# A memset moved to GpSimd and low parts moved between engines in a fused encoder block

## The chip, the cores and the metric

The kernel runs on one core of one Trainium2 chip. The metric is the device time of one execution in microseconds (us), the median of several runs. TensorE does the matrix products, VectorE and ScalarE the elementwise work, GpSimd a little of both, and SyncE issues most of the loads. Each engine has a queue of its own instructions, which run in the order that the program gives them, and waits for the others by semaphores.

## The reference, cut to what matters

One layer of a residual block on x of 512 tokens by 1024 features, all in float32:

```python
h = rms_norm(x, attn_norm_g);  z = h @ w_in
y_mla  = mla_group(...)     # 8 latent-attention heads of width 64, chunked causal mask
y_diff = diff_group(...)    # 4 differential heads of width 128:
#   logits_m = q_m @ k_m.T * 64**-0.5 + bias[head, key - query]; masked by chunks of 64 frames
#   attn = softmax(logits_0) - lam * softmax(logits_1);  o = rms_norm(attn @ v) * (1 - lam_init)
x = x + concat([y_mla, y_diff]) @ w_out
x = x + (silu(causal_conv3(h2 @ w_gate)) * (h2 @ w_up)) @ w_down      # h2 = rms_norm(x)
x = x + sigmoid(rms_norm(x) @ w_ple_gate) * (p @ w_ple_proj)          # p: 512 x 256
```

## The kernel before, in words

**Products in three parts.** Each float32 operand is held as a high part, a cast to a shorter format by ScalarE, and a low part, operand minus high part. `mm3` (lines 155 to 157) adds three TensorE products: high by high, high by low, low by high. For a weight, `load_w` loads a raw tile of 128 x 1024 (`raw`, three buffers), lets ScalarE cast it (`S.copy`, line 148) and subtracts on VectorE or, if `eng` says so, on another engine (line 149). `split` (lines 189, 190, 192, 193) does the same for other tiles. A raw buffer comes free for the next load when its low part is done.

**The order of attention.** Heads are worked through in 32 slots (8 latent heads, 4 query blocks of 128 rows each), then 16 slots (4 differential heads, 4 query blocks). In a latent slot, `mla_logits` multiplies, VectorE takes the negated row maximum (`nm`, line 562) and scales it (line 563), ScalarE takes the exponential (`pm`, line 565), `probs_T` transposes on TensorE (line 530) and copies out (`pt`, lines 533 and 535), and `mla_pv` multiplies by the values (line 575). In a differential slot VectorE adds the bias in one pass (line 667), ScalarE exponentiates (line 668), and VectorE combines the two maps (lines 672 to 674). Between these steps `pump` puts pieces of other work: the projections for the differential heads (`zd`) during the latent heads, the output projection's first half (`wo_units(0, ...)`, tiles `o`) during the differential ones. TensorE's order is that of the code; those of VectorE, ScalarE and GpSimd are set by a scheduler in this part, and by the code before the fifth slot and in the FFN.

**The bias strip.** `bias_strip` is called in the seventh slot. GpSimd builds a row of biases per head (line 593), writes it to memory, spreads it over 128 rows, and reads it back shifted by one element per row (line 598), which gives the tile `strip`, 128 x 4 x 512. Then line 599 sets a corner of it, 64 rows by 4 x 64, to a large number: the part of the mask within the diagonal block. The strip is read from the first differential slot on (line 667).

**The output projection.** `wo_units(kq, dqs, nk)` loads and splits its weights through `wo_w`. For `kq` 0 the low parts are on VectorE; for `kq` 1, whose two weights are loaded during the last latent head and the differential heads, they are on GpSimd. The last two weights (`dq` 2 and 3) take the default, VectorE. The result is added to x by VectorE (`add_x`, line 623). At a head's end `diff_pv` normalises it (`yd`, lines 688 to 698, the last of them the multiplication), and `y_split` transposes it (`yT`, line 609) for the output projection.

**p.** After attention's code, two more tiles are split into `pk`: p transposed (`pT`) and half of its projection weights (`pp0`). They go through the same raw buffers. The products that read `pk` come after the output projection.

Of the kernel before, what the change touches and what calls it, by code (L numbers as in the profile page):

```python
# [15 lines left out]
ALU = mybir.AluOpType  # L16
# [10 lines left out]
MASK = 1e30  # L27
# [62 lines left out]
def _f32(ap):  # L90
    return ap.bitcast(F32)
# [3 lines left out]
def hybrid_block(ctx: ExitStack, tc: tile.TileContext, a: dict, out: bass.AP):  # L95
    nc = tc.nc
    V, S, G, TE = nc.vector, nc.scalar, nc.gpsimd, nc.tensor
# [11 lines left out]
    def bank(tag, name):  # L109
        return pp_.tile([P, 512], F32, tag=tag, bufs={"acc": 2, "lg": 3, "tp": 2, "ob": 1}[tag], name=name)  # L110
# [4 lines left out]
    def sq_tile(name):  # L115
        return att.tile([P, D], F32, tag="sq", bufs=2, name=name)

    def pm_tile(name):
        return att.tile([P, T], F32, tag="pm", bufs=PM, name=name)
# [4 lines left out]
    def xn_tile(name):  # L124
        return keep.tile([P, D], F32, tag="xn", bufs=4, name=name)
# [7 lines left out]
    def small(name, shape, pool=None):  # L133
        return (pool or att).tile(shape, F32, name=name)
# [3 lines left out]
    def load_raw(src, n, name):  # L138
        raw = wp["rawpool"].tile([P, 1024], F32, tag="raw", bufs=wp["raw"], name=f"raw_{name}")
        nc.sync.dma_start(raw[:, :n], src)  # L140
        return raw

    def load_w(src, n, name, eng=None):

        raw = load_raw(src, n, name)
        hi = wp["pool"].tile([P, 1024], F32R, tag="hi", bufs=wp["w"], name=f"hi_{name}")
        lo = wp["pool"].tile([P, 1024], F32R, tag="lo", bufs=wp["w"], name=f"lo_{name}")
        S.copy(hi[:, :n], raw[:, :n])
        (eng or V).tensor_tensor(lo[:, :n], raw[:, :n], _f32(hi[:, :n]), op=ALU.subtract)
        return hi, lo  # L150

    def mm3(ps, blocks, first=True, last=True, again=False):
        n = len(blocks)
        for i, (xh, xl, wh, wl) in enumerate(blocks):
            TE.matmul(ps, xh, wh, start=first and i == 0, stop=False, skip_group_check=again)  # L155
            TE.matmul(ps, xh, wl, start=False, stop=False, skip_group_check=again)  # L156
            TE.matmul(ps, xl, wh, start=False, stop=last and i == n - 1, skip_group_check=again)  # L157
# [28 lines left out]
    def split(h_, l_, src, col=None, eng=None):  # L186

        if col is None:
            S.copy(h_, src)  # L189
            return (eng or V).tensor_tensor(l_, src, _f32(h_), op=ALU.subtract)  # L190
        else:
            S.activation(h_, src, AF.Identity, scale=col)
            return V.scalar_tensor_tensor(l_, src, col, _f32(h_), op0=ALU.mult, op1=ALU.subtract)
# [58 lines left out]
    for kq in range(4):  # L252
        raw = xn_tile(f"xT{kq}")
# [71 lines left out]
    raw, ukv_ = load_raw(a["w_ukv"], 1024, "ukv"), []  # L325
# [259 lines left out]
    def bias_strip():  # L585

        tab = small("tab", [DH, 32])
        nc.sync.dma_start(tab, a["rel_bias"])
        vec1 = dram.tile([DH, NR], F32, name="vec1")
        vec2 = dram.tile([P, DH, NR], F32, name="vec2")  # L590
        vb = sq_tile("vb")[:DH, :NR]
        for c0, c1, b in RUNS:
            G.tensor_scalar(vb[:, c0:c1], tab[:, b:b + 1].broadcast_to([DH, c1 - c0]), -1.0, None, op0=ALU.mult)
        nc.gpsimd.dma_start(vec1, vb)
        nc.gpsimd.dma_start(vec2, vec1.partition_broadcast(P))
        strip = att.tile([P, DH, T], F32, tag="strip", name="strip")
        skew = bass.AP(vec2.tensor, vec2.offset + 127, [[DH * NR - 1, P], [NR, DH], [1, T]])
        nc.gpsimd.dma_start(strip, skew)
        V.memset(strip[:64, :, 448:], MASK)
        strips.append(strip)  # L600


# [10 lines left out]
    def wo_blocks(k0, k1, b, w):  # L613

        c = [slice((k % 4) * 256 + (b % 2) * P, (k % 4) * 256 + (b % 2) * P + P) for k in range(k0, k1)]
        return [(w[0][:, c[i]], w[1][:, c[i]], yh[k0 + i], yl[k0 + i]) for i in range(k1 - k0)]
# [5 lines left out]
    def add_x(b, ps):  # L622
        V.tensor_tensor(xb(b), xb(b), ps, op=ALU.add)  # L623

    wo2 = {}

    def wo_w(kq, dq, eng=None):
        return load_w(a["w_out"][kq, dq], 1024, f"o{kq}{dq}", eng)

    def wo_units(kq, dqs, nk):  # L630

        for dq in dqs:
            w = wo_w(kq, dq, G if kq else V)
            if kq:
                wo2[dq] = w
            for b in (2 * dq, 2 * dq + 1):
                ps = bank("acc", f"o{kq}{b}")
                for k in range(0, nk, 2):
                    mm3(ps, wo_blocks(4 * kq + k, 4 * kq + k + 2, b, w), k == 0, k == nk - 2)
                    if k == nk - 2:  # L640
                        add_x(b, ps)
                    yield

    df = {}
# [9 lines left out]
    def diff_logits(h, t):  # L654
        n = (t + 1) * P
        if t == 0:
            df["s0", h] = sm.tile([P, NT], F32, tag="s0", name="s0")
        s0 = df["s0", h][:, t:t + 1]
        (qh_, ql_), (kh_, kl_) = df["qk", h, 0], df["qk", h, 1]
        pms, s1 = [], sm.tile([P, 1], F32, tag="s1", bufs=4, name="s1")  # L660
        for m in range(2):
            r = slice(64 * m, 64 * m + 64)
            ps = bank("lg", f"dl{h}{t}{m}")
            mm3(ps[:, :n], [(qh_[r, tsl[t]], ql_[r, tsl[t]], kh_[r, :n], kl_[r, :n])])
            pm = pm_tile("pmd")
            nm = sm.tile([P, 1], F32, tag="nm", bufs=4, name="nmd")
            V.tensor_tensor_reduce(out=pm[:, :n], in0=ps[:, :n], in1=strips[0][:, h, T - n:], scale=1.0, scalar=3e38, op0=ALU.add, op1=ALU.min, accum_out=nm)
            S.activation(pm[:, :n], pm[:, :n], AF.Exp, bias=nm, scale=-1.0, accum_out=s0 if m == 0 else s1)
            pms.append(pm)

        cf = sm.tile([P, 1], F32, tag="cf", bufs=4, name="cf")
        V.reciprocal(cf, s1)
        V.scalar_tensor_tensor(cf, cf, nlam, s0, op0=ALU.mult, op1=ALU.mult)
        V.scalar_tensor_tensor(pms[0][:, :n], pms[1][:, :n], cf, pms[0][:, :n], op0=ALU.mult, op1=ALU.add)
        df["pm", h, t] = pms[0]

    def diff_pv(h, t):
# [43 lines left out]
    for i, (h, t) in enumerate(slots):  # L721
        if i + 1 < len(slots):
            mla_logits(*slots[i + 1])
        if i == 4:
            region.__exit__(None, None, None)
        if i == 8:
            with tc.issue_after(mla["k"].ins):
                zd_norm(0)
        if h + 1 < H and t < 2:
            (mla_q, mla_k)[t](h + 1)  # L730
        if i < 3:
            zw1.append(load_w(a["w_d"][1, i + 1], 1024, f"d1{i + 1}"))
        if h < H - 1:
            pump(FILL_MLA[t])
        if i == 6:
            bias_strip()
        if h == H - 1:
            if t == 0:
                pump(100)
                fill.append(wo_units(0, range(4), 4))  # L740
            last_mla[t]()
        mla["pt", h, t] = probs_T(mla.pop(("pm", h, t)), t, f"m{h}{t}", t % 2)
        if i:
            mla_pv(*slots[i - 1])
    diff_logits(0, 0)
    mla_pv(*slots[-1])
    diff_logits(0, 1)
    pump()
    y_split(3, ymn[3], None, "tp")
    for i, (h, t) in enumerate(dslots):  # L750
        if i + 2 < len(dslots):
            diff_logits(*dslots[i + 2])
        if h + 1 < DH and t == 0:
            diff_T(h + 1, 1)
        pump(FILL_DIFF[h][t])
        df["pt", h, t] = probs_T(df.pop(("pm", h, t)), t, f"d{h}{t}", True)
        if i:
            diff_pv(*dslots[i - 1])
        if h + 1 < DH and t == 0:
            diff_T(h + 1, 0)  # L760
        if h and t == 3:
            y_split(4 + h - 1, df["y", h - 1], ocol, "tp")
            if h == 2:
                fill.append(wo_units(1, range(2), 2))
# [7 lines left out]
    for dq in (2, 3):  # L772
        wo2[dq] = wo_w(1, dq)

    pk = kvp.tile([P, 4, 1024], F32R, tag="kv", name="pk")
    for i, (src, name) in enumerate(((a["pT"], "pT"), (a["w_pp"][0], "pp0"))):
        split(pk[:, 2 * i], pk[:, 2 * i + 1], load_raw(src, 1024, name))
    ptw, wpp = (pk[:, 0], pk[:, 1]), [(pk[:, 2], pk[:, 3])]
    order = (0, 4, 1, 5, 2, 6, 3, 7)
    early = {}  # L780
    for b in order[:6]:
        n = len(early)
# [464 lines left out]
```

## Time and profile before

| | |
|---|---|
| time, median of 3 runs | 681.25 us (681.24 to 685.42) |
| profiled execution | 685.5 us, its span 683.7 us |
| TensorE busy | 654.0 us, 96% of the span |
| VectorE busy | 487.9 us, 71% |
| ScalarE busy | 358.2 us, 52% |
| GpSimd busy | 60.5 us, 9% |
| mean granted TensorE clock | 0.979 of full speed |

In the profile PE is TensorE, PEld its weight loads, DVE VectorE, ACT ScalarE, POOL GpSimd, SP SyncE; a letter q behind a name means the engine's issue queue. L599 is line 599. Rows of the time order read: start, length, engine, line, operation, output <- inputs, and in brackets how long the engine had been idle before and what released it. Rows of the list of waits read: who waited, for whom, us in total, times, longest. Rows of the chain read: start, length, engine, tile, line, where "issue" is time in which the profile shows nothing that was waited for. In tables of stretches each engine's busy time is followed by its number of instructions; the last three columns are the granted clock (1.00 is full speed), the share of the DMA engines in use, and GB/s. Attention's slots run from about 70 to 250 us, the FFN from there to the end.

### The profile page before, as it was taken

Reading aid. Unit: us, or ns where it says so; the run is one execution under the profiler, and the core shown is the slowest. Engines: PE = TensorE matmul, PEld = TensorE weight load, DVE = VectorE, ACT = ScalarE, POOL = GpSimd, SP = SyncE. Lnnn points to the kernel's source line nnn. Section 1 sums busy time; section 2 is a strip of 40 time slices with the busy share of each in tenths; the row PEclk is TensorE's granted clock in tenths of the full one; section 3 lists DMA queues with packets and bytes.
Section 4 is the critical chain, followed back from the end, with each engine's and each line's share of the span. In section 5 each row is a group of like instructions: output and inputs, shape, how many; then the busy total and the mean of one; then the engine's idle time right before and its main releaser. Section 6 shows DMA issues by size and latency. Waiting matters only on the chain.

```text
span 683.7 us, 10360 instructions
## 1 busy us (share of the span) xinstructions
PE 654.0 (96%) x3932; PEld 577.1 (84%) x3932; DVE 487.9 (71%) x941; ACT 358.2 (52%) x623; POOL 60.5 (9%) x91
## 2 busy tenths in 40 slices
PE   8999896899898999999899999999999999999997
PEld 8888785788776878688899999999999999988886
DVE  5989672646578886798867686777767676867553
ACT  6496562446456654765545555454545454646311
POOL 1910050000110000010100001100000000000000
PEclk9999998799799999999999999999999999999999
DMA  8340226105101023873755464556556463630121
GB/s 274 105 155 31 92 60 173 62 1 185 62 5 58 2 61 128 257 194 100 207 129 174 112 195 108 171 121 186 150 148 188 119 178 100 198 126 25 61 79 52
DMA packets 29913, 82.64 MB, mean 121 GB/s; under 512 B 3100, under 2 KB 4124, under 8 KB 29736
## 3 DMA queue, kind: packets, MB, share of 16 engines
q1 hardware_dynamic: 23816, 69.17, 30.4%
q0 software_dynamic: 5616, 12.33, 10.6%
q8 instruction: 31, 0.51, 0.3%
q10 hardware_dynamic: 432, 0.49, 0.2%
q14 instruction: 18, 0.15, 0.1%
HBM read 77.77 MB, written 5.52 MB: 122 GB/s over the span
## 4 chain that ended last, share of the span: by engine, by line
PE 70%; DVE 13%; ACT 8%; DMA 4%; issue 4%; POOL 0%; ACTq 0%; DVEq 0%
PE dn L157 6%; PE dn L156 6%; PE dn L155 6%; PE gx L157 4%; PE gx L156 4%; PE gx L155 4%; PE g L156 3%; PE g L155 3%; PE g L157 3%; PE mo L575 2%; PE pg L155 2%; PE pg L157 2%; PE pg L156 2%; PE zd L155 2%; PE zd L156 2%
## 5 line engine op out<-in xcount | busy, mean ns | idle before, releaser
L190 DVE TENSOR_TENSOR wSl<-rS,wSh 128x1024 fp32r<-128x1024 f32 x21 | 25.7, 1224 | 46.9 <-ACT wSh L189 46.6
L157 PE MATMUL dn<-ah,lo_dn 128*128 128x512 f32 x144 | 56.3, 391 | 0.0
L156 PE MATMUL dn<-al,hi_dn 128*128 128x512 f32 x144 | 56.2, 390 | 0.0
L155 PE MATMUL dn<-ah,hi_dn 128*128 128x512 f32 x144 | 56.1, 389 | 0.0
L884 POOL DMA_DIRECT2D rS<-in_w_gu x19 | 22.9, 1204 | 325.8 <-DVE cv L1002 114.1
L189 ACT CAST wSh<-rS 128x1024 fp32r<-128x1024 f32 x21 | 22.1, 1052 | 39.1 <-PE gy L156 39.1
L155 PE MATMUL zd<-hi_d,xh 128*128 128x512 f32 x96 | 40.3, 420 | 0.0
L156 PE MATMUL zd<-lo_d,xh 128*128 128x512 f32 x96 | 38.4, 400 | 0.0
L565 ACT ACTIVATE pm<-ml,nm,rq 128x128 f32<-128x128 f32 (+3 forms) x32 | 19.7, 617 | 29.4 <-DVE nm L563 29.4
L623 DVE TENSOR_TENSOR x<-x,dn 128x512 f32<-128x512 f32 x44 | 29.9, 680 | 6.4 <-PE dn L157 6.3
L190 DVE TENSOR_TENSOR wTl<-rA,wTh 128x1024 fp32r<-128x1024 f32 x19 | 23.3, 1226 | 15.1 <-ACT wTh L189 14.5
L157 PEld LDWEIGHTS dn<-ah,lo_dn 128*128 128x128 f32 x144 | 27.0, 188 | 5.6
L155 PEld LDWEIGHTS dn<-ah,hi_dn 128*128 128x128 f32 x144 | 27.1, 188 | 5.0
L156 PEld LDWEIGHTS dn<-al,hi_dn 128*128 128x128 f32 x144 | 27.1, 188 | 5.0
L562 DVE TENSOR_REDUCE nm<-ml 128x1 f32<-128x128 f32 (+3 forms) x32 | 15.5, 485 | 21.6 <-PE ml L157 21.5
L189 ACT CAST wAh<-rA 128x1024 fp32r<-128x1024 f32 x22 | 23.2, 1052 | 14.1 <-DMA rA<-in_w_gu 10.1
L1003 ACT ACTIVATE cv<-cv 128x512 f32<-128x512 f32 x22 | 13.9, 631 | 28.8 <-DVE cv L1002 28.8
L155 PE MATMUL g<-b2h,wAh 128*128 128x256 f32 (+1 forms) x88 | 26.4, 300 | 1.7 <-ACT g L971 1.7
L190 DVE TENSOR_TENSOR wAl<-rA,wAh 128x1024 fp32r<-128x1024 f32 x22 | 26.8, 1216 | 1.8 <-ACT wAh L189 1.8
L189 ACT CAST wTh<-rA 128x1024 fp32r<-128x1024 f32 x19 | 20.0, 1051 | 14.3 <-PE g L156 10.1
L155 PE MATMUL o<-yh,hi_o 128*128 128x512 f32 x64 | 27.1, 423 | 0.0
L530 PE MATMUL pTm<-ident,pm 128*128 128x128 f32 x80 | 15.2, 290 | 12.3 <-ACT pt L533 9.1
(469 smaller groups left out, 2271.0 us busy)
## 6 DMA issues: line engine op xcount, KB each, us to landing
rA<-in_w_gu SPq DMA_DIRECT2D x22, 512.0 KB, 3.8
rS<-in_w_gu SPq DMA_DIRECT2D x22, 512.0 KB, 3.7
rS<-in_w_gu POOLq DMA_DIRECT2D x19, 512.0 KB, 6.0
raw_dn<-in_w_down SPq DMA_DIRECT2D x18, 512.0 KB, 5.8
raw_d<-in_w_d SPq DMA_DIRECT2D x12, 512.0 KB, 3.6
r<-in_w_gu SPq DMA_DIRECT2D x19, 256.0 KB, 5.8
raw_o<-in_w_out SPq DMA_DIRECT2D x8, 512.0 KB, 3.7
rS_pg<-in_w_pg SPq DMA_DIRECT2D x6, 512.0 KB, 3.9
```

The source lines that it names most:

```text
L155: TE.matmul(ps, xh, wh, start=first and i == 0, stop=False, skip_group_check=again)
L156: TE.matmul(ps, xh, wl, start=False, stop=False, skip_group_check=again)
L157: TE.matmul(ps, xl, wh, start=False, stop=last and i == n - 1, skip_group_check=again)
L189: S.copy(h_, src)
L190: return (eng or V).tensor_tensor(l_, src, _f32(h_), op=ALU.subtract)
L530: TE.transpose(ps[:, tsl[j]], pm[:, tsl[j]], ident)
L562: V.reduce_max(nm, ps[:, :n], axis=AX.X, negate=True)
L565: S.activation(pm[:, :n], ps[:, :n], AF.Exp, bias=nm, scale=r, accum_out=mla["ssum", h // 2][:, t, h % 2:h % 2 + 1])
L575: TE.matmul(po[:, w], pt[:, tsl[j]], kv[j][:, h, 96:], start=j == 0, stop=j == t)
L623: V.tensor_tensor(xb(b), xb(b), ps, op=ALU.add)
L884: nc.gpsimd.dma_start(sums[f].rearrange("p (i c) -> p i c", i=2), a["w_gu"][f][:, :2048].rearrange("p (i c) -> p i c", i=2)[:, :, :512], a ...
L1003: S.activation(cv, cv, AF.Silu)
```

## The change

Three edits. The strip's corner is set by GpSimd instead of VectorE. All low parts of the output projection's weights are computed on VectorE. The low parts of p and its weights are kept behind the last `scalar_tensor_tensor` of the softmax (line 674, last head, last block) by `issue_after`, which tells the scheduler to place what stands in its block behind the named instruction; their casts on ScalarE are written apart and are free.

```diff
-        V.memset(strip[:64, :, 448:], MASK)
+        G.memset(strip[:64, :, 448:], MASK)
...
-    def wo_w(kq, dq, eng=None):
-        return load_w(a["w_out"][kq, dq], 1024, f"o{kq}{dq}", eng)
+    def wo_w(kq, dq):
+        return load_w(a["w_out"][kq, dq], 1024, f"o{kq}{dq}")
...
-            w = wo_w(kq, dq, G if kq else V)
+            w = wo_w(kq, dq)
...
-        V.scalar_tensor_tensor(pms[0][:, :n], pms[1][:, :n], cf, pms[0][:, :n], op0=ALU.mult, op1=ALU.add)
+        df["last"] = V.scalar_tensor_tensor(pms[0][:, :n], pms[1][:, :n], cf, pms[0][:, :n], op0=ALU.mult, op1=ALU.add)
...
-        split(pk[:, 2 * i], pk[:, 2 * i + 1], load_raw(src, 1024, name))
+        raw = load_raw(src, 1024, name)
+        S.copy(pk[:, 2 * i], raw)
+        with tc.issue_after(df["last"].ins):
+            V.tensor_tensor(pk[:, 2 * i + 1], raw, _f32(pk[:, 2 * i]), op=ALU.subtract)
```

TensorE's order and SyncE's order of transfers stay as they are. The others change in the following places (numbers behind a name tell one buffer of it from the next).

VectorE in the ninth latent slot: `nm<-ml_1259` is the row maximum of the first block of the third head, `lo_d` the low part of a projection weight.

```order
 L563 TENSOR_TENSOR nm<-nm,rq 128x1
 L535 COPY pt<-pTm_1251 128x384
-L599 MEMSET strip 64x4x64
 L562 TENSOR_REDUCE nm<-ml_1259 128x1
 L149 TENSOR_TENSOR lo_d_1379<-raw_d_1376,hi_d_1378 128x1024
```

The memset leaves VectorE's queue; on GpSimd it stands last before the FFN's transfers, directly behind the transfer at line 598, where the two subtractions stood.

VectorE at the start of the last latent head: `lo_o_2574` is the first of the two low parts that GpSimd had; `nm<-ml_1771` belongs to that head's first block.

```order
 L535 COPY pt<-pTm_1763 128x384
 L563 TENSOR_TENSOR nm<-nm,rq 128x1
+L149 TENSOR_TENSOR lo_o_2574<-raw_o_2571,hi_o_2573 128x1024
 L562 TENSOR_REDUCE nm<-ml_1771 128x1
 L563 TENSOR_TENSOR nm<-nm,rq 128x1
```

The low part comes between the scaling of one block's maximum and the next block's maximum. The second one, `lo_o_2655`, comes likewise in front of the first addition (line 667) of the second differential head's second map.

ScalarE in the second differential head: `pk<-raw_pT` is the cast of p, `pt<-pTd` copies of transposed maps, `st<-d1T` the cast of the next head's keys.

```order
 L668 ACTIVATE pmd,s_2059<-pmd,nmd 128x128
+L533 COPY pt<-pTd_2094 128x384
 L668 ACTIVATE pmd,s_2060<-pmd,nmd 128x128
-L533 COPY pt<-pTd_2094 128x384
 L668 ACTIVATE pmd,s_2059<-pmd,nmd 128x256
 L668 ACTIVATE pmd,s_2102<-pmd,nmd 128x256
-L189 CAST pk<-raw_pT 128x1024
 L533 COPY pt<-pTd_2130 128x512
-L189 CAST st<-d1T_2161 128x512
+L778 CAST pk<-raw_pT 128x1024
 L668 ACTIVATE pmd,s_2059<-pmd,nmd 128x384
```

The cast of p moves behind one copy and ahead of the cast of the keys. Its low part leaves VectorE's queue in this head, and the one of p's weights does so in the next step; both now stand in the last head, behind the last row of line 674 and ahead of the multiplication that ends the third head (`yd_2593`):

```order
 L174 SCALAR_TENSOR_TENSOR ro<-rs_t,ro 128x4
 L176 SCALAR_TENSOR_TENSOR rs_g<-rs_t,rs_g 128x4
-L173 SCALAR_TENSOR_TENSOR rs_t<-rs_g,ro 128x4
-L174 SCALAR_TENSOR_TENSOR ro<-rs_t,ro 128x4
+L780 TENSOR_TENSOR pk<-raw_pT,pk 128x1024
+L173 SCALAR_TENSOR_TENSOR rs_t<-rs_g,ro 128x4
+L623 TENSOR_TENSOR x_1865<-x_1865,o_2666 128x512
+L174 SCALAR_TENSOR_TENSOR ro<-rs_t,ro 128x4
+L780 TENSOR_TENSOR pk<-raw_pp_2745,pk 128x1024
 L698 TENSOR_TENSOR yd_2593<-yd_2593,ro 128x512
-L623 TENSOR_TENSOR x_1865<-x_1865,o_2666 128x512
 L193 SCALAR_TENSOR_TENSOR yh6l<-yT_2692,ocol,yh_2697 128x512
```

Ahead of `yd_2593` stand now both low parts and one addition to x that had stood behind it.

## The prediction

> **What bounds the kernel now.** The page first: how busy is TensorE, and where is its clock not full?
>
> ```profile
> PE 654.0 (96%) x3932; PEld 577.1 (84%) x3932; DVE 487.9 (71%) x941; ACT 358.2 (52%) x623; POOL 60.5 (9%) x91
> PEclk9999998799799999999999999999999999999999
> ```
>
> TensorE bounds the kernel. A slice is 17.1 us long, and the granted clock reads below 9 in slices 7 and 8 (103 to 137 us) and 11 (171 to 188): all in attention, where all three edits lie too. So the second view is the list of waits: what does TensorE wait for longest, and who waits for a transfer?
>
> ```profile
> DVE strip L599 <- DMA strip<-vec: 10.5, 1, 10.5
> PE pTm L530 <- ACT pt L533: 9.1, 2, 8.9
> PE pTd L530 <- ACT pt L533: 0.9, 1, 0.9
> ```
>
> TensorE's longest wait, 8.9 us, is put down to a copy of ScalarE's (L533); VectorE's longest, 10.5, to the strip's transfer. Whether they are one and the same, the chain must tell. Third, the table by stretches: the 8.9 us wait, one of 3.13, two small ones, and behind each the time at a lowered clock (columns: us, then busy time of TensorE, its weight loads, VectorE, ScalarE and GpSimd, then the granted clock).
>
> ```profile
> 112.92:121.80 8.88, 0.00 (x0) 0.00 (x1) 2.44 (x6) 1.59 (x5) 0.80 (x1) 0.65 0.46 134
> 121.80:129.15 7.35, 7.35 (x25) 6.42 (x26) 5.19 (x16) 4.46 (x9) 0.00 (x0) 0.50 0.32 117
> 170.61:173.74 3.13, 0.01 (x1) 0.00 (x0) 2.54 (x4) 0.92 (x3) 2.16 (x1) 0.99 0.52 205
> 173.74:183.95 10.21, 10.21 (x44) 9.72 (x45) 3.45 (x8) 3.73 (x10) 0.00 (x0) 0.50 0.18 52
> 208.08:211.30 3.22, 1.23 (x10) 1.04 (x10) 2.78 (x6) 2.42 (x6) 0.00 (x0) 0.99 0.13 25
> 211.30:214.65 3.35, 3.35 (x12) 2.18 (x13) 2.22 (x7) 2.96 (x7) 0.00 (x0) 0.50 0.32 132
> ```
>
> Each gap is followed by a stretch at clock 0.50 in which TensorE is busy throughout. A gap therefore costs twice: its own length, and half of the slow stretch behind it.
>
> **The strip's memset.** The chain of waits around the first gap:
>
> ```profile
> 108.04 10.46 issue
> ...
> 118.56 0.27 DVE strip L599
> 118.83 0.14 DVE nm L562
> 118.98 1.12 DVE lo_d L149
> 120.10 0.08 DVE nm L563
> 120.21 0.55 ACT pm L565 x2
> 120.75 0.52 ACT sq L395
> 121.27 0.48 ACT pt L533
> 121.80 0.47 PE pTm L530
> ```
>
> VectorE stands still for 10.46 us in front of L599. Behind it in VectorE's queue stand the row maximum and its scaling (L562, L563), behind those ScalarE's exponential and copy (L565, L533), and behind those TensorE's transposes (L530): the two waits are one. With L599 gone from VectorE, the chain from 118.83 to 121.80, 2.97 us long, starts at 108.04 and ends near 111.0. TensorE gets there at 112.92, so 1.9 us are to spare for whatever ScalarE has queued, and the 8.88 us go. The slow stretch goes with them: 7.35 us at half speed are 3.68 too many, since TensorE had work for all of it. **Term A: -12.6 us** (-8.9 if the later work turns out to wait for other engines at full speed).
>
> On GpSimd the memset waits for the same transfer; behind it in that queue stand only the FFN's transfers. The strip's first reader, and the nearest memset on GpSimd:
>
> ```profile
> 188.07 0.29 DVE L667 CUSTOM_DVE_ANT_0 pmd<-dl,strip 128x128 f32<-128x128 f32 x1 [0.46 <-PE dl L157]
> 0.72 0.20 POOL masks.py:197 MEMSET ident<- 128x128 f32 x1 [0.29 <-POOLq L1239]
> ```
>
> The strip's memset writes twice as much per partition, so some 0.4 us, done near 119; the reader comes at 188.07 less A and B, near 169, with 50 us to spare. Should it hold VectorE up for its length, it costs those 0.4, or 2.3 if it is as slow as GpSimd's subtraction below. I take 0.
>
> **The output projection's low parts.** The second gap, in the last latent head, with the same low part on VectorE for comparison (last row):
>
> ```profile
> 170.43 2.34 POOL L149 TENSOR_TENSOR lo_o<-raw_o,hi_o 128x1024 fp32r<-128x1024 f32 x1 [56.70 <-ACT hi_o L148]
> 170.66 2.12 DVE L563 TENSOR_TENSOR nm<-nm,rq 128x1 f32<-128x1 f32 x1
> 172.82 0.78 ACT L565 ACTIVATE pm<-ml,nm,rq 128x512 f32<-128x512 f32 x1 [2.47 <-DVE nm L563]
> 173.74 1.12 PE L530 MATMUL pTm<-ident,pm 128*128 128x128 f32 x4 [3.13 <-ACT pm L565]
> 162.88 1.23 DVE L149 TENSOR_TENSOR lo_o<-raw_o,hi_o 128x1024 fp32r<-128x1024 f32 x1 [1.89 <-ACT hi_o L148]
> ```
>
> The scaling of one column, 0.08 us in the chain above, takes 2.12 here and ends with GpSimd's subtraction: VectorE is held up by it. In the new order the low part stands on VectorE behind this scaling and ahead of the next row maximum. ScalarE's cast, for which it waits, is done at 170.43, as GpSimd's start shows, so nothing is held up by that. The exponential then starts near 170.8, some 2.05 us earlier, and 3.13 - 2.05 = 1.08 us of the gap remain. The next row maximum starts when the low part ends, near 172.0; its exponential is due about 2 us behind the first, so I put nothing on it. If 1.08 us doesn't lower the clock, half of 10.21 = 5.1 goes as well, less 0.5, my guess for softmax waits that full speed uncovers where no fill work is left. **Term B: -2.05 - 4.6 = -6.7** (from -2.1 to -7.2).
>
> Does 1.08 us lower the clock? The slow stretches last 3.35 and 10.21 us, one and three times about 3.41. So I cut the run into windows of 3.41, in phase with the changes of the grant:
>
> ```profile
> 81.52:84.93 3.41, 2.19 (x19) 1.95 (x18) 3.41 (x6) 0.88 (x1) 0.00 (x0) 1.00 0.32 96
> 207.81:211.23 3.42, 1.48 (x11) 1.03 (x9) 2.77 (x6) 2.62 (x6) 0.00 (x0) 1.00 0.12 22
> ```
>
> After the first, with TensorE busy for 2.19 us, the clock stayed full; after the second, with 1.48, it fell. A wait of 1.08 leaves 2.33: safe by these rows.
>
> **p's low parts, taken away.** The third gap, in the second differential head:
>
> ```profile
> 201.30 2.38 POOL L149 TENSOR_TENSOR lo_o<-raw_o,hi_o 128x1024 fp32r<-128x1024 f32 x1 [28.52 <-ACT hi_o L148]
> 203.70 0.33 SPq L140 DMA_DIRECT2D raw_pT<-in_pT  x1
> 207.38 1.05 ACT L189 CAST pk<-raw_pT 128x1024 fp32r<-128x1024 f32 x1 [1.83 <-DMA raw_pT<-in_pT]
> 208.33 0.58 ACT L533 COPY pt<-pTd 128x512 f32<-128x512 f32 x1
> 211.30 1.12 PE L649 MATMUL d0T<-ident,zd 128*128 128x128 f32 x4 [1.11 <-DVE st L190]
> ```
>
> The load of p is issued when GpSimd's second low part frees its buffer; ScalarE waits 1.83 us for it, and the copy that TensorE needs stands behind the cast. On VectorE that low part ends near 202.5, the load, which took 3.7, lands near 206.2, and the copy now stands ahead of the cast: the 0.9 us wait goes. VectorE loses p's first low part here and gains this one. The cast still stands in ScalarE's queue ahead of this head's exponentials, with VectorE's and TensorE's next steps behind them, so I keep 1.1 us of wait in front of the transposes at 211.30, which come 0.95 earlier. One wait of 1.1 leaves 2.3 busy in its window, so the slow stretch, half of 3.35, goes. The second load, of p's weights, now takes a buffer that VectorE frees; its cast stands some steps later and I put nothing on it. **Term C: -0.95 - 1.7 = -2.6** (from 0 to -3.7).
>
> **p's low parts, put back.** They now stand behind the last softmax row's L674, ahead of L698:
>
> ```profile
> 249.50 0.69 DVE L698 TENSOR_TENSOR yd<-yd,ro 128x512 f32<-128x512 f32 x1
> 250.84 0.60 PE L609 MATMUL yT<-ident,yd 128*128 128x128 f32 x4
> L155 PE MATMUL pp<-pk x8: 389/391/476, 269.7 to 276.1; 128*128 128x512 f32 x8
> ```
>
> L698 was done at 250.19, 0.65 before the transposes at 250.84 that read it. Two low parts (1.12 each, as lo_d in the chain) and one addition of L698's size (0.6) now come first: 250.19 + 2.24 + 0.6, less 0.2 for gaps between tiny instructions that get filled, is 252.8. TensorE takes its queue in order, so it waits 1.9 us, and all of the output projection behind it moves by as much. The parts themselves aren't read before 269.7. A wait of 1.9 within one window leaves 1.5 of 3.41 busy, as in the window that lost the clock; the work behind is dense, as behind 211.30, where one window brought it back: 1.7 more. **Term D: +1.9 + 1.7 = +3.6** (from 0 to +7.0, which is 1.9 and half of 10.21).
>
> Here a page is weighed. The Trainium skill, "TensorE: Matmul & The Clock Gate", section "HAM oscillation — how this bites in real kernels", gives as the rule that only TensorE gaps above about 3.4 us are to be avoided. By it D would lose no clock, and the sum would end 1.7 lower. The trace speaks against it: a window with 1.48 us of work, whose longest single wait was 1.11, was followed by half clock. I go by the row.
>
> **Sum.** The profiled execution took 685.5 us, 1.8 beside its span of 683.7. 685.5 - 12.6 - 6.7 - 2.6 + 3.6 = **667.2**. The median shown is 681.25, or 4.25 less than the profiled run. The slow stretches cost half of 20.9 = 10.5 us there, and I take the difference to be some of their windows, which end with the gaps in either case. So the time after is the same, and the gain on the median is 14, about 2.1%.
>
> **Rivals.**
> - The clock survives D, since a gap below 3.4 us doesn't lower it, or since the wait is split over two windows: 665.5. For it: 1.9 is near the edge, and where the windows fall is open. The page's rule above would have it so. Chance 0.30.
> - New waits take the place of B and C: with the low parts on VectorE the clock falls at 171 and 210 as before. Then 4.6 + 1.7 come back: 673.5. For it: waits of 1.1 remain there by my own count, and 0.15 us more would leave the range that the rows cover (2.19). Chance 0.17.
> - The change doesn't do it: the first gap stays, since a load or ScalarE's queue holds the same chain as long. 667.2 + 12.6 = 679.8. Against it: from 118.83 to 121.80 the chain runs without a pause. Chance 0.05.
> - Slower: VectorE becomes the bound of the differential heads.
>
> ```profile
> 200.00:250.00 50.00, 47.44 (x286) 37.30 (x285) 42.65 (x148) 31.11 (x80) 2.38 (x1) 0.97 0.07 22
> ```
>
> It is busy for 42.65 of 50 us there. If TensorE waits for it once per head as in D (1.9) and each time loses the clock for three windows as after 173.74 (5.1), four heads cost 28, against 21.9 gained: 691.6. It decides from where TensorE's work in a window falls to about 1.5. Against it: only one low part (1.23) is new to this stretch; the other two move within it. Chance 0.03.
>
> **How the numbers follow.** The forecast keeps 0.45. The range, 663 to 675, takes in the first two rivals, and below the sum the 3.6 of D at nothing; 8 in 100 lie outside by the cases, the rest of the 2 in 10 is for errors of size in A to C. A measurement of this kernel tells about 1% from no change. Faster by more are the forecast and the first two rivals, less the part of the second that ends beyond 674.4: 0.89. Same 0.08, slower 0.03.
>
> **What would show it.** In the changed kernel's profile: no wait of VectorE for the strip, TensorE's 8.9 us wait gone, the memset on GpSimd within 1 us of its transfer's end (A); L563 at its 0.1 to 0.2 us everywhere, and full clock in slice 11 (B); no wait of ScalarE for p ahead of a copy (C); TensorE waiting for L698 by some 1.9 us near 229 us (250.84 - 21.9), with a lowered clock behind it (D). I am wrong if a TensorE wait above 3 us is left before 200 us, if the clock falls at the remaining waits of 1.1, or if VectorE's low parts wait for ScalarE's casts with softmax behind them.

## The result, and the profile after

The changed kernel takes **663.89 us** (median of 4 runs, 663.66 to 663.94) against 681.25 for the kernel before (681.11 to 685.42). The ratio is 0.9733, with a 95% interval of 0.9701 to 0.9764. Its profiled execution took 663.66 us with a span of 661.9, against 685.5 and 683.7 before: 21.8 us between the two profiles, 17.4 between the medians. The prediction was 667, with a range of 663 to 675.

The page of the changed kernel, the rows of TensorE and of the granted clock:

```profile
PE 643.0 (97%) x3932; PEld 567.8 (86%) x3932; DVE 487.2 (74%) x942; ACT 358.3 (54%) x623; POOL 56.5 (9%) x90
PEclk9999999999999999999999999999999999999999
```

No slice lies below 9 any more: the half-clock stretches of slices 7, 8 and 11 are gone. The 8.9 us wait is no longer in the list of TensorE's waits. The time order around its old place (start, length, engine, line, operation):

```profile
108.02 0.29 DVE L562 TENSOR_REDUCE nm<-ml 128x1 f32<-128x128 f32 x1 [0.18 <-PE ml L157]
112.54 0.27 PE L530 MATMUL pTm<-ident,pm 128*128 128x128 f32 x1
...
118.92 0.31 POOL L599 MEMSET strip<- 64x256 f32 x1 [5.30 <-DMA strip<-vec]
```

The row maximum starts at 108.02 and TensorE's transpose at 112.54, without a wait. The memset now waits for the strip on GpSimd, takes 0.31 us at 118.92, and nobody stands behind it.

The second gap:

```profile
157.89 0.15 DVE L563 TENSOR_TENSOR nm<-nm,rq 128x1 f32<-128x1 f32 x1
157.96 1.22 DVE L149 TENSOR_TENSOR lo_o<-raw_o,hi_o 128x1024 fp32r<-128x1024 f32 x1
158.08 0.78 ACT L565 ACTIVATE pm<-ml,nm,rq 128x512 f32<-128x512 f32 x1 [0.50 <-DVE nm L563]
159.00 0.66 PE L530 MATMUL pTm<-ident,pm 128*128 128x128 f32 x4 [1.16 <-ACT pm L565]
```

L563 is back at 0.15 us (2.12 before), the low part follows on VectorE, and 1.16 of the 3.13 us remain. The third gap, in the second differential head:

```profile
181.67 1.23 DVE L149 TENSOR_TENSOR lo_o<-raw_o,hi_o 128x1024 fp32r<-128x1024 f32 x1
182.93 0.33 SPq L140 DMA_DIRECT2D raw_pT<-in_pT  x1
185.72 0.57 ACT L533 COPY pt<-pTd 128x512 f32<-128x512 f32 x1
186.39 1.05 ACT L778 CAST pk<-raw_pT 128x1024 fp32r<-128x1024 f32 x1
189.33 0.66 PE L649 MATMUL d0T<-ident,zd 128*128 128x128 f32 x4
```

p's load is issued as VectorE's low part ends. The copy stands ahead of the cast, ScalarE waits for neither, and the transposes `d0T` start without any wait (1.11 before). The fourth place, behind the last softmax row:

```profile
225.21 1.22 DVE L780 TENSOR_TENSOR pk<-raw_pT,pk 128x1024 fp32r<-128x1024 f32 x1
227.09 1.22 DVE L780 TENSOR_TENSOR pk<-raw_pp,pk 128x1024 fp32r<-128x1024 f32 x1
228.22 0.68 DVE L698 TENSOR_TENSOR yd<-yd,ro 128x512 f32<-128x512 f32 x1
229.05 0.63 PE L609 MATMUL yT<-ident,yd 128*128 128x128 f32 x4 [1.78 <-DVE yd L698]
```

Both low parts stand ahead of L698, and TensorE waits 1.78 us. The table by stretches shows what the clock made of it (columns: us; busy time of TensorE, weight loads, VectorE, ScalarE, GpSimd; granted clock):

```profile
226.24:229.65 3.41, 1.62 (x16) 1.46 (x14) 2.66 (x6) 0.62 (x2) 0.00 (x0) 1.00 0.43 154
229.65:233.07 3.42, 3.13 (x18) 2.44 (x17) 2.38 (x9) 1.76 (x3) 0.00 (x0) 1.00 0.45 133
```

The clock stays full.

### The profile page after: what moved, and what is told of

Same layout as the page of the kernel before. It is cut to its first block, busy times and chain, and to the rows that moved or that the text cites. A ratio compares the mean times of both kernels' runs of the same rounds, so it can differ in the third digit from the quotient of the medians.

```text
span 661.9 us, 10359 instructions
## 1 busy us (share of the span) xinstructions
PE 643.0 (97%) x3932; PEld 567.8 (86%) x3932; DVE 487.2 (74%) x942; ACT 358.3 (54%) x623; POOL 56.5 (9%) x90
## 4 chain that ended last, share of the span: by engine, by line
PE 68%; DVE 15%; ACT 8%; DMA 5%; issue 3%; ACTq 0%; DVEq 0%
PE dn L157 6%; PE dn L156 6%; PE dn L155 6%; PE gx L157 4%; PE gx L156 4%; PE gx L155 4%; PE g L156 3%; PE g L155 3%; PE g L157 3%; PE mo L575 2%; PE pg L155 2%; PE pg L157 2%; PE pg L156 2%; PE u L155 2%; PE u L157 2%
## 5 line engine op out<-in xcount | busy, mean ns | idle before, releaser
L190 DVE TENSOR_TENSOR wSl<-rS,wSh 128x1024 fp32r<-128x1024 f32 x21 | 25.7, 1225 | 46.9 <-ACT wSh L189 46.7
L190 DVE TENSOR_TENSOR wTl<-rA,wTh 128x1024 fp32r<-128x1024 f32 x19 | 23.3, 1224 | 14.5 <-ACT wTh L189 13.9
L190 DVE TENSOR_TENSOR wAl<-rA,wAh 128x1024 fp32r<-128x1024 f32 x22 | 26.8, 1216 | 1.6 <-ACT wAh L189 1.6
L157 PE MATMUL g<-b2h,wAl 128*128 128x256 f32 (+1 forms) x88 | 26.2, 297 | 0.0
```

## The experiments

Between the same TensorE rows of two traces the time can be compared stretch by stretch, whatever happened earlier. Four stretches serve for all runs: from the transposes `kT` near 72 us to the first four `pTm` of the last latent head (the first gap, and the second gap's wait); from there to `d0T` of the third differential head (half clock behind the second gap, p's load and casts); from there to `yT` of the third head (half clock behind the third gap, the wait for L698); and the rest. In us, from the profiled executions (the last column from spans given to a tenth):

| kernel | kT to pTm | pTm to d0T | d0T to yT | yT to end |
|---|---|---|---|---|
| before | 100.61 | 37.56 | 39.54 | 432.9 |
| changed | 86.08 | 30.33 | 39.72 | 432.9 |
| changed, other chip | 86.08 | 30.29 | 39.74 | 432.5 |
| strip alone | 88.05 | 37.21 | 39.54 | 432.3 |
| low parts alone | 97.56 | 30.46 | 38.39 | 432.7 |
| p alone | 99.30 | 36.16 | 39.80 | 433.1 |
| all but p | 86.07 | 30.35 | 38.42 | 432.5 |
| p behind yd | 86.11 | 30.55 | 37.80 | 433.2 |
| p's first low part repeated | 86.06 | 33.80 | 39.70 | 433.2 |
| both of p's repeated | 86.08 | 30.40 | 39.83 | 433.8 |
| memset late on VectorE | 86.11 | 30.49 | 39.89 | 432.9 |
| GpSimd reads | 86.10 | 31.82 | 39.86 | 432.7 |
| GpSimd writes | 86.06 | 30.47 | 39.73 | 432.4 |

What lies ahead of `kT` differs by about 2 us between runs (it starts at 71.0 to 73.1), and is no part of this comparison.

### The edits one by one

Theory: each edit removes its own wait and the half clock behind it, and the edits add up. Rival: work that comes earlier runs into the next wait, so that they share one gain. Four kernels on one chip, where the kernel before took 681.69 us.

**The strip alone.**

```diff
-        V.memset(strip[:64, :, 448:], MASK)
+        G.memset(strip[:64, :, 448:], MASK)
```

> Only the strip's corner moves to GpSimd; all else as before. Theory (each edit removes its own wait and half of the slow stretch behind it, and the edits do not touch each other): the first gap goes with its 7.35 us at half clock, -12.6, so 668.7 from the median of 681.25 (672.9 from the profiled 685.5); the gaps of 3.1 us (lo_o on GpSimd) and before d0T stay, TensorE's longest wait is 3.1. Rival (work that comes earlier runs into the next wait, so the edits share one gain): part of the 8.9 us comes back at the second gap, 672 to 677 from the median, and that gap is longer than 3.1.

Measured: 670.52 us, ratio 0.9824 (0.9792 to 0.9856). The first stretch shrank by 12.56, the figure of term A. The other two gaps stood as before, each with its half clock:

```profile
156.26:159.39 3.13, 0.00 (x1) 0.00 (x1) 2.54 (x4) 0.92 (x3) 2.16 (x1) 0.94 0.39 153
159.39:169.24 9.85, 9.85 (x42) 9.36 (x43) 3.09 (x8) 3.73 (x10) 0.00 (x0) 0.50 0.18 53
193.14:196.55 3.41, 1.64 (x11) 1.03 (x9) 2.78 (x6) 2.62 (x6) 0.00 (x0) 1.00 0.24 29
196.60:199.96 3.36, 3.36 (x12) 2.19 (x13) 2.23 (x7) 2.96 (x7) 0.00 (x0) 0.50 0.31 124
```

The second gap is 3.13 us to the hundredth: nothing was handed on to it. So the rival falls by the trace; the time alone, between the 668.7 of the theory and the 672 of the rival, would not decide. The third stands with the wait that it had before, in the list of waits:

```profile
PE d0T L649 <- DVE st L190: 1.1, 1, 1.1
```

**The low parts alone.**

```diff
-            w = wo_w(kq, dq, G if kq else V)
+            w = wo_w(kq, dq)
```

> Only the output projection's low parts move to VectorE; strip's memset and p's low parts as before. Theory: the first gap of 8.9 us stays; L563 is back at 0.1 to 0.2 us and the second gap shrinks to about 1.1 with full clock behind it, -6.8; p's load is issued some 1.2 us earlier, and the wait before d0T shrinks or goes, 0 to -3.8. From the median 671 to 674.5. Rival (the wait before d0T goes only because of the third edit): it stays at about 1 us with its slow stretch, 674.5.

Measured: 673.14 us, ratio 0.9872 (0.9837 to 0.9907). In the time order:

```profile
192.73 0.33 SPq L140 DMA_DIRECT2D raw_pT<-in_pT  x1
195.52 0.56 ACT L533 COPY pt<-pTd 128x512 f32<-128x512 f32 x1
196.33 1.05 ACT L189 CAST pk<-raw_pT 128x1024 fp32r<-128x1024 f32 x1 [0.24 <-DMA raw_pT<-in_pT]
199.27 0.66 PE L649 MATMUL d0T<-ident,zd 128*128 128x128 f32 x4
```

ScalarE waits 0.24 us for p (1.83 before), the copy is ahead of the cast, and `d0T` waits for nobody. The second stretch is 7.1 us shorter, as in the full change (7.2). All that term C was to bring comes with this edit.

GpSimd's second subtraction had held VectorE up in the kernel before as well: L673, 0.22 us in the changed kernel, took 1.09 there and ended with it (203.69 and 203.68).

```profile
202.60 1.09 DVE L673 SCALAR_TENSOR_TENSOR cf<-cf,nlam,s 128x1 f32<-128x1 f32 x1
```

VectorE stood idle for 0.81 and 1.46 us after that, the second time for the cast of p, so the chain to `d0T` ran through p's load. No run here separates the earlier load from the freed VectorE.

**p alone.**

```diff
-        V.scalar_tensor_tensor(pms[0][:, :n], pms[1][:, :n], cf, pms[0][:, :n], op0=ALU.mult, op1=ALU.add)
+        df["last"] = V.scalar_tensor_tensor(pms[0][:, :n], pms[1][:, :n], cf, pms[0][:, :n], op0=ALU.mult, op1=ALU.add)
...
-        split(pk[:, 2 * i], pk[:, 2 * i + 1], load_raw(src, 1024, name))
+        raw = load_raw(src, 1024, name)
+        S.copy(pk[:, 2 * i], raw)
+        with tc.issue_after(df["last"].ins):
+            V.tensor_tensor(pk[:, 2 * i + 1], raw, _f32(pk[:, 2 * i]), op=ALU.subtract)
```

> Only p's low parts are queued behind the last softmax row; strip and output projection as before. Theory: the wait for L698 is there, +2.0; before d0T TensorE now waits for ScalarE's copy and not for VectorE's low part, which stands behind d0T, but p's load still waits for GpSimd's low part, so ScalarE's 1.8 us wait for it stays: between 0 and -3.8 there. From the median 679.4 to 683.3. Rival (the buffer that d0T gets is what freed it): the wait before d0T goes here too, 679.4, the low end of it; by the theory that the earlier load freed it, the high end.

Measured: 682.43 us, ratio 1.0016 (1.0000 to 1.0032): no gain. The wait for L698 is there (1.8). Before `d0T`:

```profile
203.43 1.05 ACT L778 CAST pk<-raw_pT 128x1024 fp32r<-128x1024 f32 x1 [1.76 <-DMA raw_pT<-in_pT]
204.38 0.58 ACT L533 COPY pt<-pTd 128x512 f32<-128x512 f32 x1
206.85 0.66 PE L649 MATMUL d0T<-ident,zd 128*128 128x128 f32 x4 [0.61 <-ACT pt L533]
```

The cast still waits 1.76 us for p, with the copy behind it. Alone, this edit halves the wait before `d0T` (0.61, for a copy and no longer for VectorE's L190), and the clock stayed full behind it; the wait for L698 takes that back.

**All but p**, which is the first two edits together.

```diff
-        V.memset(strip[:64, :, 448:], MASK)
+        G.memset(strip[:64, :, 448:], MASK)
...
-            w = wo_w(kq, dq, G if kq else V)
+            w = wo_w(kq, dq)
```

> The strip's memset and the output projection's low parts as in the change; p's low parts stay where they were before. Theory (the third edit as a whole costs the wait for L698 and brings nothing, since p's earlier load alone frees the copy ahead of d0T): 661.9, no wait for L698, no wait before d0T. Rival (the third edit brings the wait before d0T down): a wait of about 1.1 us and perhaps a slow window there, 663.0 to 665.7.

Measured: 661.12 us, ratio 0.9697 (0.9663 to 0.9731). The second stretch is that of the full change (30.35 and 30.33), the third 1.30 us shorter. So the second edit frees `d0T` without the third, and in company of the other two the third edit costs 1.3 us by the trace. The measured times can't tell that: the intervals of the two ratios overlap.

The ratios of the three single edits come to -12.0, -8.7 and +1.1 us, -19.6 together; the full change's ratio is -18.2 on the first chip (0.9733) and -19.4 on another (0.9716, below). With intervals of 1 to 2.4 us either way on each of these ratios, they add up.

### Place or engine

The memset back on VectorE, some 40 instructions further on; no other instruction moves.

```diff
-        G.memset(strip[:64, :, 448:], MASK)
...
+        if i == 20:
+            with tc.issue_after(mla["k"].ins):
+                V.memset(strips[0][:64, :, 448:], MASK)
```

> The change, except that the strip's memset is on VectorE again, but later in its queue: 41 instructions further on, in the sixth latent head, when the strip has long landed. No other instruction changes its place. Theory (the first gap came from the place of a waiting instruction in VectorE's in-order queue, not from the engine that does the memset): no wait, the memset takes about 0.3 us there, and the time is that of the change within 0.5 us, a ratio to the kernel before of 0.970 to 0.976. Rival (the engine matters: VectorE has no room for it, or the strip's consumer then waits): 12.6 us more or part of it, a ratio of 0.98 to 0.992.

```profile
127.58 0.27 DVE L738 MEMSET strip<- 64x256 f32 x1
```

Measured: 663.25 us, ratio 0.9736 (0.9697 to 0.9775), with the first stretch at 86.11. The memset ran without a wait, long after the strip had landed (117.03 in this trace). The 12.6 us belonged to the place of a waiting instruction in an in-order queue; the engine had no part in it.

### What GpSimd's subtraction does to VectorE

To the changed kernel one instruction on GpSimd is added in the last latent head, with a one-column copy on ScalarE that starts it. Nobody reads its result. It is a subtraction in one kernel (`s` is the strip seen as 128 x 2048), and in the other `G.memset(jg, 0.0)` in place of the last line.

```diff
+            if t == 1:
+                jg = sq_tile("jg")
+                S.copy(jg[:, :1], mla["pm", h, t][:, :1])
+                G.tensor_tensor(jg, s[:, :1024], s[:, 1024:], op=ALU.subtract)
```

> The change, with one added subtraction of 128x1024 on GpSimd (two operands of the strip, a result that nobody reads), started by a one-column copy of ScalarE in the last latent head, near 162 us. Nobody waits for it. Theory (a GpSimd instruction that reads two operands from SBUF holds VectorE's instructions with two SBUF operands up for its whole length): a VectorE instruction of that stretch, L563 (0.16 us in the change) or a low part of 0.7, takes 1.5 to 2.4 us, the softmax behind it comes late, TensorE waits 1 to 3 us there, and with a fallen clock up to 5 more: 1 to 7 us above the change. Rival (before, L563 waited for something else that ended at the same moment): VectorE's instructions keep their lengths, 0 to +0.3.

> The same as the kernel with the added subtraction, but GpSimd's added instruction is a memset of the same 128x1024 tile: it writes as much and reads nothing. Theory (only GpSimd's reading side competes with VectorE): L563 and the low parts keep their lengths, 0 to +0.3 above the change. Rival (any SBUF access of GpSimd holds VectorE up): the same wait as with the subtraction, as long as the memset takes.

The subtraction, then the memset, in the time order:

```profile
162.28 2.37 POOL L745 TENSOR_TENSOR jg<-strip 128x1024 f32<-128x1024 f32 x1 [41.50 <-issue]
162.81 1.85 DVE L563 TENSOR_TENSOR nm<-nm,rq 128x1 f32<-128x1 f32 x1
165.32 0.66 PE L609 MATMUL yT<-ident,ym 128*128 128x128 f32 x4 [1.13 <-DVE st L190]
```

```profile
161.05 0.96 POOL L745 MEMSET jg<- 128x1024 f32 x1 [42.41 <-ACT jg L744]
161.66 0.16 DVE L563 TENSOR_TENSOR nm<-nm,rq 128x1 f32<-128x1 f32 x1
```

Under the subtraction L563 lasts 1.85 us and ends when GpSimd does (164.65), and TensorE waits 1.13 us that it didn't wait before; the stretch from `pTm` to `d0T` is 1.5 us longer than in the changed kernel. Under the memset L563 keeps its 0.16. The times (663.94 and 663.98, ratios 0.9730 and 0.9735) don't tell 1.5 us apart; the traces do. The Trainium skill, "SBUF — State Buffer", section "Who interferes with whom", says that a VectorE instruction with two SBUF inputs contends with a GpSimd instruction that reads SBUF and not with one that only writes it: 1.85 and 0.16 us agree with it.

### p's low parts where VectorE idles

The changed kernel unaltered, for comparison on the same chip, and the changed kernel with `df["last"]` set at L698 instead of L674.

```diff
-        df["last"] = V.scalar_tensor_tensor(pms[0][:, :n], pms[1][:, :n], cf, pms[0][:, :n], op0=ALU.mult, op1=ALU.add)
+        V.scalar_tensor_tensor(pms[0][:, :n], pms[1][:, :n], cf, pms[0][:, :n], op0=ALU.mult, op1=ALU.add)
...
-        V.tensor_tensor(yv, yv, ro.unsqueeze(2).broadcast_to([P, NT, P]), op=ALU.mult)
+        df["last"] = V.tensor_tensor(yv, yv, ro.unsqueeze(2).broadcast_to([P, NT, P]), op=ALU.mult)
```

> The changed kernel itself, unaltered, as the common measure of the three below on one chip: 660 to 664 by where its start falls (TensorE's work began 1.3 to 1.5 us earlier in the runs of the single edits than in the profile of the change).

> The change, with p's low parts issued behind the last head's L698 (yd), where VectorE idles 3.99 us, and not ahead of it. Theory (the wait for L698 is all that the third edit costs, and nobody needs p's low parts before p's product): the 1.8 us wait goes, 1.8 below the changed kernel of the same chip, about 0.4 below the change without its third edit. Rival (the wait is not VectorE's queue but what is ahead of it, or the low parts then hold up yh7l's low part and the residual's additions): 0 to -0.5, with a wait of TensorE for VectorE near 237 us.

Line 698 runs once per head, and its last run sets what the low parts stand behind: the multiplication of the last head. In the changed kernel VectorE idles there for 3.97 us:

```profile
237.76 0.75 DVE L193 SCALAR_TENSOR_TENSOR yh7l<-yT,ocol,yh 128x512 fp32r<-128x512 f32 x1 [3.97 <-ACT yh L192]
```

With the low parts moved, the multiplication of the third head, then that of the last:

```profile
224.43 0.69 DVE L698 TENSOR_TENSOR yd<-yd,ro 128x512 f32<-128x512 f32 x1
225.77 0.60 PE L609 MATMUL yT<-ident,yd 128*128 128x128 f32 x4
...
230.64 0.69 DVE L698 TENSOR_TENSOR yd<-yd,ro 128x512 f32<-128x512 f32 x1
231.25 1.22 DVE L780 TENSOR_TENSOR pk<-raw_pT,pk 128x1024 fp32r<-128x1024 f32 x1
232.39 1.22 DVE L780 TENSOR_TENSOR pk<-raw_pp,pk 128x1024 fp32r<-128x1024 f32 x1
```

The wait for L698 is gone, and the third stretch is 37.80 us: 1.94 less than in the changed kernel, 0.62 less than without the third edit. Not all of it is kept. From `kT` to the end this kernel takes 587.7 us, the changed kernel 588.6 and the one without the third edit 587.3. In the rest, TensorE waits 1.15 us for a cast of ScalarE's in the FFN (`b1h`), and 0.55 and 0.51 in the other two. The chain ahead of that wait runs through a transfer (`pps<-ppo`) of 6.77 us here and of 6.13 and 6.09 there; whether the low parts have a part in that isn't shown. Measured: 660.84 us, ratio 0.9711 (0.9684 to 0.9737), against 662.41 and 0.9716 (0.9701 to 0.9731). Two of its five runs lie near 664.2 and three near 660.5. So the trace shows that the wait is gone, and neither trace nor timing shows a gain over the kernel without the third edit.

### A longer wait, and the clock

A repeat of p's first low part, and of both, was to lengthen the wait for L698.

```diff
             V.tensor_tensor(pk[:, 2 * i + 1], raw, _f32(pk[:, 2 * i]), op=ALU.subtract)
+            if i == 0:     # in the other kernel, for both
+                V.tensor_tensor(pk[:, 2 * i + 1], raw, _f32(pk[:, 2 * i]), op=ALU.subtract)
```

> The change, with p's first low part computed twice ahead of L698, so that TensorE's wait for yd grows by 1.1 to 2.9 us. By the windows of 3.41 us (the clock falls where the work in one is about 1.5 or less): up to 1.9 of idle leaves the clock, so 2.9 drops it unless a boundary cuts it into 1.0 to 1.9 on both sides (about one phase in four): the clock falls to half in most runs, +1.1 for the wait and +1.7 or more for each half-clock window, 2.8 to 6 above the changed kernel in all. By the rule that only a gap above 3.4 us counts: full clock, +1.1.

> The change, with each of p's two low parts computed twice ahead of L698: TensorE's wait is about 4.1 us. Both rules let the clock fall: +2.3 for the wait and one to three windows at half clock (1.7 each), 4.0 to 7.4 above the changed kernel. If it stays full, +2.3, both are wrong.

Measured: 663.30 us (ratio 0.9728, 0.9713 to 0.9742) and 664.33 (0.9746, 0.9724 to 0.9768). Neither did what it was for. With one repeat:

```profile
228.67 1.21 DVE L782 TENSOR_TENSOR pk<-raw_pT,pk 128x1024 fp32r<-128x1024 f32 x1
229.81 0.68 DVE L698 TENSOR_TENSOR yd<-yd,ro 128x512 f32<-128x512 f32 x1
230.41 1.21 DVE L780 TENSOR_TENSOR pk<-raw_pp,pk 128x1024 fp32r<-128x1024 f32 x1
```

The repeat (L782) took the place of the second low part, and that one went behind L698: the wait stayed at 1.80 in both kernels. With two repeats, two subtractions went behind it, ahead of the low part of the third head's result, and TensorE waited for that one:

```profile
PE o L156 <- DVE yh6l L193: 1.1, 1, 1.1
```

Neither run answers what a longer wait for L698 does to the clock. But the first of them showed something else, at the second gap, where its code is that of the changed kernel. Its row and the half clock behind it, then the same window of the kernel without the third edit:

```profile
155.30:158.71 3.41, 2.26 (x21) 2.12 (x20) 2.37 (x6) 2.11 (x5) 0.00 (x0) 1.00 0.52 201
158.71:165.54 6.83, 6.83 (x30) 6.34 (x29) 3.03 (x7) 2.96 (x9) 0.00 (x0) 0.50 0.18 72
```

```profile
155.30:158.72 3.42, 2.27 (x22) 2.13 (x21) 2.72 (x6) 2.12 (x4) 0.00 (x0) 1.00 0.62 244
158.72:162.13 3.41, 3.41 (x29) 3.34 (x29) 2.27 (x6) 2.31 (x7) 0.00 (x0) 1.00 0.52 154
```

The same wait of 1.15 us, the same window from 155.30 on, the same work in it: once the clock fell for 6.83 us, once it didn't. Three more kernels (the changed one on the other chip, the low parts alone, p behind yd) have this wait in a window with 2.26 us of work, and there too the clock stayed full. How much work runs at half clock behind one and the same gap varies as well. Behind the first gap it was 7.35 us in the kernel before, and 4.44 with p alone:

```profile
111.20:120.17 8.97, 0.00 (x1) 0.01 (x2) 2.44 (x6) 1.60 (x5) 0.79 (x1) 0.68 0.44 132
120.17:124.61 4.44, 4.44 (x18) 4.19 (x19) 2.46 (x6) 3.52 (x7) 0.00 (x0) 0.50 0.23 92
167.56:170.69 3.13, 0.00 (x2) 0.01 (x1) 2.53 (x4) 0.92 (x3) 2.16 (x1) 0.73 0.30 120
170.69:179.22 8.53, 8.53 (x38) 8.43 (x39) 2.60 (x7) 3.07 (x9) 0.00 (x0) 0.50 0.23 61
```

The last two rows are the second gap and the half clock behind it: 8.53 us of work here, 10.21 before. Here the clock had already fallen within the gap, whose mean grant is 0.73 against 0.99 before; so part of the half clock fell on idle time.

## Why the prediction came out as it did

Shifts of TensorE between the profiles of before and after, place by place, against the terms:

| term | predicted | measured |
|---|---|---|
| A, strip | -12.6 | -12.6 |
| B, output projection's low parts | -6.7 | -6.8 |
| C, p's low parts taken away | -2.6 | -3.8 |
| D, p's low parts put back | +3.6 | +2.0 |
| the rest | 0 | -0.6 |
| sum | -18.3 | -21.8 |

The time came out 3.3 us below the 667.2 of the sum, 0.9 above the lower end of the range; on another chip the same kernel took 662.41, just under that end. C and D together were 2.8 us too high.

- **A held, step for step.** The chain from VectorE's row maximum to the transposes ran as soon as the memset was off its path, the 1.9 us to spare were enough, and both halves of the term (the wait, and half of the 7.35 us) came back. The late memset on VectorE shows the reason itself: it was a waiting instruction with softmax behind it.
- **B held.** L563 went from 2.12 to 0.15 us, 1.16 us of the gap remained where 1.08 was worked out, and the clock stayed full. That GpSimd's reading held VectorE up, which the prediction read from one coincidence of ends, the added subtraction shows. One part was right by good fortune: "safe by these rows" is not so. Among the ten profiled executions with this remaining wait the clock fell in one, after a window with 2.26 us of work.
- **C: the step that failed is "I keep 1.1 us of wait in front of the transposes at 211.30".** It was argued that the cast still stands ahead of ScalarE's exponentials. It does; but ScalarE had been late by the 1.83 us that it stood waiting for p, and without them the 1.05 us of the cast fit. Nothing of the wait was left: 1.2 us more than the term. That the gain comes with p's earlier load was named rightly, as far as the chain shows; the run with the low parts alone shows that it came from the second edit. The prediction priced the load under the third. It overlooked that GpSimd's second subtraction held VectorE up as well (L673, 1.09 us), though it read this of the first one.
- **D: the wait was right (1.9 predicted, 1.78 measured), the lost clock was not.** The step that failed is "A wait of 1.9 within one window leaves 1.5 of 3.41 busy, as in the window that lost the clock", for which 1.7 us were added. The window held 1.62 us of work, and in all eight profiled executions with this wait (1.78 to 1.83 us) the clock stayed full. In six of them the wait lies within one window, of 1.61 to 1.63 us of work; in the other two a boundary cuts it. This is the first rival, at 665.5.
- **The clock rules.** The Trainium skill, "TensorE: Matmul & The Clock Gate", section "HAM oscillation — how this bites in real kernels", has as its rule that gaps above about 3.4 us are to be avoided. For D, full clock came out, as by that rule. For the rest the runs speak against it: waits of 3.13 us and of 1.1 were each followed by half clock in the kernel with the strip alone. The prediction's own reading, by the work in a window, is no better: windows with 1.64 and 2.26 us fell, one with 1.62 did not. What decides is open.
- **The other rivals.** The waits of 1.1 that were to cost the clock at B and C did so at B in one execution of ten; the first gap did not stay; VectorE did not bound the differential heads.
- **Profile and median.** The prediction took the 4.25 us by which the profiled run of before lay above its median to be windows of half clock. The runs bear out that the work at half clock varies for the same gap (7.35 and 4.44 us behind the first, 10.21 and 8.53 behind the second); half of these differences makes 2.3 us. The rest wasn't traced to a place.

## What to carry to other kernels

Look in each engine's queue for an instruction that waits for a transfer and ask what stands behind it; here moving it, on its own engine or to another, was worth the wait and half of the slow clock behind (12.6 us). When work is taken off a queue, ask whether the engine there was late or only waiting: what it stood idle for is available to all that follows. When work is put back, look for the stretch in which its new engine idles, and not only for the last moment at which nothing needs the result: two low parts ahead of the third head's multiplication cost a wait of 1.8 us. Two subtractions right behind it cost one of 1.06, and behind the last head's multiplication, where VectorE idles, TensorE waited for neither.

## What the runs showed of the hardware that was not expected

- The TensorE work that the trace shows in a window did not decide the granted clock. A window of 3.41 us with 2.26 us of work was followed by half clock in one execution, by full clock in four others. In the unaltered changed kernel on another chip the clock fell once at 23.69 us, after a window with 3.18 us of work:

```profile
20.28:23.69 3.41, 3.18 (x24) 3.17 (x24) 2.93 (x10) 0.96 (x3) 3.25 (x7) 1.00 0.34 95
23.69:27.11 3.42, 3.42 (x12) 3.24 (x11) 3.21 (x11) 1.38 (x3) 3.27 (x3) 0.50 0.12 48
```

- Half clock comes in whole windows: 3.41 us here, 6.83 behind the 1.15 us wait. Those 6.83 us made the stretch around them 3.4 to 3.5 us longer than in the changed kernel and in the kernel with both parts repeated (33.80 against 30.29 to 30.40), so one window cost about 1.7 us. Executions of one kernel differ by more: with p behind yd two of 664.1 and 664.4 us had a mean clock of 0.992 and 0.991, three of 660.1 to 660.8 one of 0.996 to 0.999. So a change worth 1.3 to 1.9 us is read from the traces here; the times don't show it.
